# One decoder layer on one core: norm chains of two token tiles, inputs laid out by quarters, and squares added ahead of a sum

## The chip, the core and the metric

The kernel runs on one core of a Trainium2 chip. TensorE (PE in the profile, with its weight loads as PEld) multiplies, VectorE (DVE), ScalarE (ACT) and GpSimd (POOL) do the elementwise work, and SyncE (SP) issues nearly all transfers. The metric is the device time of one launch in microseconds. The kernel before took 1597.15 us, the median of three runs (1595.09 to 1598.02).

## The reference, cut to what matters

The layer has x of 1024 tokens by 1024 columns, in fp32. Only its first stage is touched by most of the change, and the query norm of the memory attention by one line.

```python
def rms_norm(x, gain=None):
    y = x * lax.rsqrt(jnp.mean(x * x, axis=-1, keepdims=True) + EPS)
    return y if gain is None else y * gain

h = rms_norm(x, norm_mix)
rq, rk, rv, rg, dq, dk, dv = split(h @ w_in)
# retention, 8 heads: rotary(rq), rotary(rk), chunks of 128 tokens -> o_ret
dq = rms_norm(dq, diff_q_gain)      # per token and map, 64 columns
dk = rms_norm(dk, diff_k_gain)      # 4 heads, 2 maps each
s  = causal(dq @ dk.T) / 8          # two maps per head
a  = softmax(s[0]) - lam * softmax(s[1])
o_diff = rms_norm(a @ dv, diff_subln) * 0.8
x = x + (concat(o_ret, o_diff) * group_scale) @ w_out

h, m = rms_norm(x, norm_x), rms_norm(mem, norm_mem)
q, (k, v) = h @ xq, split(m @ xkv)
q, k = rms_norm(q, xq_gain), rms_norm(k, xk_gain)   # 4 heads of 256 columns
x = x + softmax(q @ k.T / 16) @ v @ xo
h = rms_norm(x, norm_ffn)
x = x + (silu(h @ w_gate) * (h @ w_up)) @ w_down
```

## The kernel before, in words

Every fp32 operand of a large product is split into a high part, rounded to fp32r by a copy (names with h), and a low part, the rest (names with l). A product is three matmuls, high by high, high by low and low by high (`mm3`). The gain of the first norm goes into the transposed input xT when it is split (`split_x`). The norm's root, one number per token (`rstd`), is not multiplied into xT: it is applied behind the projection.

The projection and both attentions run as one sequence of 64 items, eight groups of eight token tiles (128 tokens each): d0, r0, d1, r1, d2, r2, d3, r3, where d is a differential head (class `Diff`) and r a pair of retention heads (class `Ret`). The loop over n does the attention of item n (`m1`, and the transposes and products of the item before in `m2` and `m3`) and the projection of item n + 4 (`gemm`, in four parts). Between them stand the norm of the queries and keys of a differential tile (`e1`) and the transpose of its keys (`e3`). `e1` sums squares of the keys on ACT and DVE and those of the queries with a matmul by `ones` (tile dss), and then runs `rsqrt`, a chain of 13 DVE instructions on at most 16 columns in which nearly each waits for the one before. Its results are in dsm; rx_d, ry_d and rw_d are the chain's other tiles, rx_x, ry_x and rw_x those of the tokens' root.

Before the loop the kernel loads the input twice: transposed by quarters of 256 tokens, in halves of four blocks (`load_xT`, tiles xs), and by tokens (`load_x`), to get the tokens' root (`token_norm`). For quarters 2 and 3 POOL multiplies the gain in ahead of the split.

All matmuls stay in program order. Where `keep_in_program_order` stands, the other engines do too; elsewhere a scheduler sets an engine's order by priority, and `tc.high_priority()` moves what stands under it ahead. Each engine works through its own queue in that order, so an instruction that waits holds back all behind it. PSUM has two buffers each for projections (mm), scores (S) and small products (ms).

After the loop come the output projection, the memory attention in 16 steps (xG projects two tiles of queries of one head, xR sums their squares and runs `rsqrt`, xS scores, xT_, xO, xX), and the feed-forward part.

## Time and profile before

| | before |
|---|---|
| median of three runs | 1597.15 us |
| profiled execution, its own time | 1599.99 us |
| its span | 1598.2 us |
| mean granted TensorE clock | 0.989 |
| PE busy | 1537.0 us, 96% of the span |
| DVE busy | 1026.7 us, 64% |
| ACT busy | 621.3 us, 39% |
| POOL busy | 280.9 us, 18% |

The profiled execution's own time is 1.8 us above its span, and 2.84 us above the median of the runs. PE is busy nearly everywhere, so the table alone says little: what a change of another engine is worth is read from the stretches in which PE waits for that engine. The page's slices show where these are: the first two slices of 40 (to about 80 us) have the lowest PE share, 6 and 8 tenths, while DVE is at 8 and 9. A granted clock below 1 in a stretch means that matmuls there ran in part at 1.2 instead of 2.4 GHz.

### The profile page before, as it was taken

The page shows a single profiled execution, that of the slowest core. Times are in us where ns is not written, and L with a number is a line of the kernel's source. Part 1 is how long each engine was busy: PE and PEld are TensorE (multiplying, and loading weights), DVE is VectorE, ACT ScalarE, POOL GpSimd, SP SyncE. Part 2 cuts the span into 40 slices and gives each one's busy share as a digit, 9 for nine tenths or more (in the row PEclk, how much of TensorE's full clock was granted, in tenths as well). Part 3 has the DMA queues.
Part 4 walks back from the last instruction along what each step waited for, and adds up shares of the span by engine and source line. Part 5 has one row for each costly group of instructions (what it writes and reads, how often), then busy time and mean ns, then how long its engine had stood idle before and what let it go on. Part 6 is the DMA issues. An engine that isn't in the chain of part 4 may idle for free.

```text
span 1598.2 us, 23419 instructions
## 1 busy us (share of the span) xinstructions
PE 1537.0 (96%) x8782; PEld 1323.4 (83%) x8782; DVE 1026.7 (64%) x2519; ACT 621.3 (39%) x1200; POOL 280.9 (18%) x400
## 2 busy tenths in 40 slices
PE   6899999999999999999999969999999999899999
PEld 6778878888888988899999958888888888688887
DVE  8954864963876734755555886767676666555554
ACT  6442442442445722333332453333333333343332
POOL 3423323322312122111121230000000000000000
PEclk9999999999999999899999999999999999999999
DMA  8201111110103652100001122444444444788562
GB/s 293 73 27 46 39 40 41 40 46 27 41 27 137 208 183 80 40 27 27 27 27 42 79 93 86 152 151 152 163 153 161 166 162 158 250 299 260 199 219 83
DMA packets 69234, 180.85 MB, mean 113 GB/s; under 512 B 7425, under 2 KB 12929, under 8 KB 69121
## 3 DMA queue, kind: packets, MB, share of 16 engines
q1 hardware_dynamic: 68112, 178.81, 31.7%
q8 instruction: 69, 1.13, 0.3%
q10 hardware_dynamic: 1008, 0.55, 0.1%
q14 instruction: 45, 0.36, 0.1%
HBM read 135.55 MB, written 43.78 MB: 112 GB/s over the span
## 4 chain that ended last, share of the span: by engine, by line
PE 80%; DVE 14%; ACT 2%; issue 2%; DMA 1%; POOL 0%; ACTq 0%; SPq 0%; DVEq 0%; POOLq 0%
PE x L64 15%; PE g_r L64 8%; PE z L64 7%; PE dx L64 7%; PE dy L64 6%; PE xo L64 5%; PE wo L64 5%; PE xq L64 5%; PE y L64 4%; PE kv L64 3%; PE xkv L64 2%; PE q L64 2%; PE av L64 2%; DVE nmx L52 2%; DVE dsm L52 1%
## 5 line engine op out<-in xcount | busy, mean ns | idle before, releaser
L64 PE MATMUL g_r<-uh_r,xT 128*128 128x512 f32 x512 | 178.2, 406 | 0.0
L52 DVE TENSOR_TENSOR dl<-ds,dh 128x1024 fp32r<-128x1024 f32 x77 | 94.0, 1224 | 95.4 <-PE dy L64 38.9
L52 ACT CAST dh<-ds 128x1024 fp32r<-128x1024 f32 x77 | 81.0, 1055 | 126.2 <-PE dx L64 63.4
L64 PE MATMUL x<-Bh,f 128*128 128x512 f32 (+1 forms) x368 | 113.7, 381 | 1.2 <-DVE G L52 1.2
L64 PEld LDWEIGHTS g_r<-uh_r,xT 128*128 128x128 f32 x512 | 96.4, 188 | 22.1 <-issue 2.4
L64 PE MATMUL kv<-uh_d,xT 128*128 128x256 f32 x512 | 110.2, 298 | 1.8 <-DVE dql L52 1.8
L52 POOL TENSOR_TENSOR G<-G,U 128x512 f32<-128x512 f32 (+1 forms) x23 | 33.9, 1474 | 395.1 <-ACT f L52 335.1
L52 DVE TENSOR_TENSOR f<-s,f 128x512 fp32r<-128x512 f32 x86 | 70.0, 814 | 50.3 <-ACT f L52 47.4
L64 PE MATMUL g_r<-ul_r,xT 128*128 128x512 f32 x256 | 100.4, 392 | 0.0
L52 ACT CAST f<-s 128x512 fp32r<-128x512 f32 x88 | 54.6, 621 | 115.6 <-DVE s L52 112.9
L64 PE MATMUL xq<-hT,uh_xq 128*128 128x256 f32 x512 | 93.0, 284 | 0.0
L64 PEld LDWEIGHTS kv<-uh_d,xT 128*128 128x128 f32 x512 | 86.2, 195 | 4.5 <-DVE dql L52 2.0
L64 PE MATMUL xo<-uh_xo,xoT 128*128 128x512 f32 x256 | 88.3, 405 | 1.1 <-DVE xr L52 1.1
L52 ACT ACTIVATE p<-s,nmx,dsm 128x128 f32<-128x128 f32 (+7 forms) x64 | 53.2, 831 | 90.1 <-DVE nmx L52 89.2
L64 PEld LDWEIGHTS x<-Bh,f 128*128 128x128 f32 x368 | 68.5, 188 | 14.9 <-DVE G L52 1.8
L64 PEld LDWEIGHTS xq<-hT,uh_xq 128*128 128x128 f32 x512 | 79.8, 191 | 0.1
L64 PE MATMUL kv<-ul_d,xT 128*128 128x256 f32 x256 | 73.6, 287 | 1.1 <-DVE ul_d L52 1.1
L64 PE MATMUL xq<-hT,ul_xq 128*128 128x256 f32 x256 | 72.6, 284 | 0.0
L52 DVE TENSOR_TENSOR G<-x,G 128x512 f32<-128x512 f32 (+1 forms) x69 | 45.7, 663 | 41.8 <-ACT G L52 38.4
L64 PE MATMUL dx<-dl,dh 128*128 128x512 f32 x176 | 68.8, 391 | 2.2 <-DVE dl L52 2.2
L64 PE MATMUL x<-Bl,f 128*128 128x512 f32 (+1 forms) x184 | 69.9, 380 | 0.0
L64 PE MATMUL dx<-dh 128*128 128x512 f32 x176 | 68.7, 390 | 1.1 <-ACT dh L52 1.1
(330 smaller groups left out, 4202.4 us busy)
## 6 DMA issues: line engine op xcount, KB each, us to landing
gu<-in_w_dram SPq DMA_DIRECT2D x21, 1024.0 KB, 6.0
ds<-gF_d SPq DMA_DIRECT2D x77, 256.0 KB, 3.9
wd<-in_w_dram SPq DMA_DIRECT2D x22, 512.0 KB, 5.5
wT_d<-wd SPq DMA_DIRECT2D x22, 512.0 KB, 3.0
ds<-wT_d SPq DMA_DIRECT2D x44, 256.0 KB, 4.1
ds<-in_w_dram SPq DMA_DIRECT2D x33, 256.0 KB, 5.2
st_r<-in_w_dram SPq DMA_DIRECT2D x16, 512.0 KB, 3.2
st_kv<-in_w_dram SPq DMA_DIRECT2D x16, 512.0 KB, 3.8
```

Source lines behind the costliest of these rows:

```text
L52: r = f(*args, **kw)
L64: return tc.keep_in_program_order(nc.tensor.matmul(*args, **kw))
```

## The change

It has four parts.

1. `e1` runs once for two tiles, on eight columns in place of four, and takes its whole chain and the scaling of the keys under `high_priority`. The tokens' root is no longer in it: the norm of a projection does not depend on a factor per token except through EPS, so the chain adds EPS times (mean square of the token + EPS), kept in `epsu`, where it multiplied by `rstd2` and `rstd`. The scaling of the values by `rstd` becomes a step of its own (`e2`), one POOL instruction for two tiles. `e3` does two tiles at once.
2. `token_norm` becomes `token_sum` (ACT's sums of squares and one DVE instruction for `epsu`), and one `rsqrt` over all eight tiles stands in the loop at n = 0. The loads of r0's weights move from n = 0 to n = 1 and 2.
3. The transposed input lies in memory as eight contiguous blocks, one per quarter and half. Its loads and the first weights' keep their order, the first ACT work is a copy of a zeroed tile, the first weight is split in two halves, the high parts of d0's other two weights move from DVE to ACT and one low part from DVE to POOL. POOL's multiplication by the gain goes; all four quarters are split by `activation` and `scalar_tensor_tensor` with the gain.
4. In the memory attention DVE adds the two halves of the queries' squares, and the sum of squares takes two matmuls in place of four.

```diff
-    def rsqrt(ss, n, mean, name, src=None):
+    def rsqrt(ss, n, mean, name, src=None, eps=None):
...
+        if eps is None:
+            ve.tensor_scalar(out=xh, in0=src, scalar1=-0.5 * mean, scalar2=-0.5 * EPS, op0=ALU.mult, op1=ALU.add)
+            ve.tensor_scalar(out=ss, in0=src, scalar1=mean, scalar2=EPS, op0=ALU.mult, op1=ALU.add)
+        else:
+            s3 = ss.rearrange("p (t c) -> p t c", t=2)
+            ve.scalar_tensor_tensor(out=s3, in0=s3, scalar=mean, in1=bc(eps, n // 2), op0=ALU.mult, op1=ALU.add)
+            ve.tensor_scalar(out=xh, in0=ss, scalar1=-0.5, scalar2=None, op0=ALU.mult)
...
-        sp.dma_start(xst[q, j], a["xT"][:, 4 * j:4 * j + 4, 256 * q:256 * q + 256])
-        if q > 1:
-            g = bc(gains[:, G_MIX + 4 * j:G_MIX + 4 * j + 4], 256)
-            for i in range(4):
-                tc.keep_in_program_order(gp.tensor_tensor(out=xst[q, j][:, i:i + 1], in0=xst[q, j][:, i:i + 1],
-                                                          in1=g[:, i:i + 1], op=ALU.mult))
+        tc.keep_in_program_order(nc.sync.dma_start(st, a["xT"][2 * q + j]))
...
-    def token_norm(q):
+    def token_sum(q):
+
         for t in (2 * q, 2 * q + 1):
             xt = xnt.pop(t)
             sc.activation(xt, xt, AF.Square, accum_out=rstd[:, t:t + 1])
-        sl = rstd[:, 2 * q:2 * q + 2]
-        with tc.high_priority():
-            rsqrt(sl, 2, 1.0 / D, f"x{q}")
-        ve.tensor_tensor(out=rstd2[:, 2 * q:2 * q + 2], in0=sl, in1=sl, op=ALU.mult)
+        sl = slice(2 * q, 2 * q + 2)
+        ve.tensor_scalar(out=epsu[:, sl], in0=rstd[:, sl], scalar1=EPS / D, scalar2=EPS * EPS,
+                         op0=ALU.mult, op1=ALU.add)
...
+    gp.memset(Rs[0], 0.0)
+    sc.copy(Rs[1], Rs[0])
+    st0 = raw("st_d0_0")
+    tc.keep_in_program_order(nc.sync.dma_start(st0, a["w"][U_DIF]))
+    w0 = [[uqp.tile([P, 1024], F32R, tag="w", name=f"u{x}_d0_0") for x in "hl"]]
     for j in range(2):
         load_xT(0, j, raw)
+        hi, lo = (t[:, 512 * j:512 * j + 512] for t in w0[0])
+        sc.copy(hi, st0[:, 512 * j:512 * j + 512])
+        low(ve, lo, st0[:, 512 * j:512 * j + 512], hi)
         split_x(0, j)
-    w0 += [unit(U_DIF + i, f"d0_{i}", eng=ve, heng=ve, stage=t4) for i in (1, 2)]
+    w0 += [unit(U_DIF + i, f"d0_{i}", eng=ve if i == 1 else gp, stage=t4, by=ordered) for i in (1, 2)]
...
+            two = slice(t - 1, t + 1)
+            kn = self.kv[:, two, 0:P]
+            for e in range(2):
+                pe.matmul(sp_[:, 2 * e:2 * e + 2], self.q[t // 2][2][:, e * P:e * P + P], ones[:, 0:2],
+                          start=True, stop=True)
...
+            with tc.high_priority():
+                rsqrt(ss, 8, 1.0 / 64, f"d{nm}", eps=epsu[:, two])
+                for e in range(2):
+                    k3 = self.kv[:, t - 1 + e, 0:P].rearrange("p (a d) -> p a d", d=64)
+                    ve.tensor_tensor(out=k3, in0=k3, in1=bc(s3[:, e, 0:2], 64), op=ALU.mult)
+
+        def e2(self, t):
+            if t % 2 == 0:
+                return
+            v = self.kv[:, t - 1:t + 1, P:2 * P]
+            gp.tensor_tensor(out=v, in0=v, in1=bc(rstd[:, t - 1:t + 1], P), op=ALU.mult)
...
         gemm(n + LEAD, (0,))
-        call("e1", n + LEAD - (1 if n else 2))
+        if n % 2 == 0:
+            call("e1", n + LEAD - 1)
+            if n:
+                call("e2", n + LEAD - 1)
         gemm(n + LEAD, (1,))
+        if n % 2:
+            call("e3", n + LEAD - 2)
         if n == 0:
-            call("e3", 0)
-            call("e3", 1)
+            token_sum(2)
+            token_sum(3)
             split_x(3, 1)
-            call("e1", 3)
-            token_norm(3)
+            rsqrt(rstd, NT, 1.0 / D, "x")
+            call("e2", 1)
+            call("e2", 3)
...
-            ws[1] = [load_part(*order[1], i) for i in range(4)]
+        if n in (1, 2):
+            ws.setdefault(1, []).extend(load_part(*order[1], 2 * n - 2 + i) for i in range(2))
...
-        call("e3", n + LEAD - 2)
...
         sc.activation(sq, ps, AF.Square)
+        ve.tensor_tensor(out=sq[:, 0:256], in0=sq[:, 0:256], in1=sq[:, 256:512], op=ALU.add)
...
-            for i in range(2):
-                pe.matmul(sp_[:, e:e + 1], sq[:, 256 * i + e * P:256 * i + e * P + P], ones[:, 2:3],
-                          start=i == 0, stop=i == 1)
+            pe.matmul(sp_[:, e:e + 1], sq[:, e * P:e * P + P], ones[:, 2:3], start=True, stop=True)
```

Three places show how the instructions stand now. The first is ACT's queue at the start of the program, before. uh_d_0 is the high part of the first weight, xs_0 and xs_1 are the halves of the first quarter.

```order
5 L52 DMA tab<-in_tab_dram 128x512
6 L52 DMA causal<-in_causal_dram 128x128
7 L52 DMA zeta<-in_zeta_dram 128x8
8 L52 ACT_TABLE_LOAD
9 L52 CAST uh_d_0_112<-st_d_0_110 128x1024
10 L52 ACTIVATE xT_106<-xs_0_116,gains 128x256 x4
11 L52 ACTIVATE xT_106<-xs_1_126,gains 128x256 x4
12 L52 ACTIVATE negI<-ident 128x128
```

The same queue in the changed program, where R is the zeroed tile:

```order
3 L52 ACT_TABLE_LOAD
4 L52 COPY R_111<-R_110 128x128
5 L52 DMA ones<-in_ones_dram 128x3
6 L52 DMA ident<-in_ident_dram 128x128
7 L52 CAST uh_d_0_116<-st_d_0_114 128x512 x2
8 L52 DMA tab<-in_tab_dram 128x512
9 L52 ACTIVATE xT_106<-xs_0_118,gains 128x256 x4
10 L52 ACTIVATE xT_106<-xs_1_130,gains 128x256 x4
11 L52 CAST uh_d_1_144<-st_d_1_142 128x1024
```

The table load stood directly ahead of the first weight's cast, which needs a transfer; now it stands ahead of a copy that needs none, and the cast of the second weight has come into ACT's queue.

The second place is DVE's queue in group d1, where the norm of tile 4 begins, before. The names with _4 are its chain; aT, rz, cf and p belong to the attention of tiles 0 and 1, and rss and rx_r to the end of retention group r0.

```order
462 L52 TENSOR_REDUCE dsm_4_2247<-dks_4_2248 128x2
463 L52 COPY dsm_4_2247<-dss_4_2245 128x2
464 L52 COPY aT_0_2278<-pt_0_0_2279 128x128
465 L52 TENSOR_SCALAR dsm_4_2247<-dsm_4_2247,rstd_109 128x4
466 L52 RECIPROCAL rz_1_2206<-Z_1_2205 128x2
467 L52 TENSOR_SCALAR rx_d_4_2253<-dsm_4_2247 128x4
468 L52 TENSOR_SCALAR rx_r_2289<-rss_2083 128x16
469 L52 SCALAR_TENSOR_TENSOR cf_1_2207<-Z_1_2205,neglam,rz_1_2206 128x1
470 L52 TENSOR_SCALAR dsm_4_2247<-dsm_4_2247 128x4
471 L52 TENSOR_SCALAR rss_2083<-rss_2083 128x16
```

The chain of tiles 4 and 5 at the same place of the changed program:

```order
325 L52 TENSOR_TENSOR nmx_2_2077<-nmx_2_2077,dsm_3_1917 128x1
326 L52 COPY dsm_5_2118<-dss_5_2115 128x2x2
327 L52 SCALAR_TENSOR_TENSOR dsm_5_2118<-dsm_5_2118,epsu 128x8
328 L52 TENSOR_SCALAR rx_d_5_2123<-dsm_5_2118 128x8
329 L52 TENSOR_SCALAR ry_d_5_2124<-dsm_5_2118 128x8
330 L52 TENSOR_SCALAR ry_d_5_2124<-ry_d_5_2124 128x8
331 L52 TENSOR_TENSOR rw_d_5_2125<-ry_d_5_2124 128x8
332 L52 TENSOR_TENSOR rw_d_5_2125<-rw_d_5_2125,rx_d_5_2123 128x8
333 L52 RECIPROCAL rz_2_2079<-Z_2_2078 128x2
334 L52 SCALAR_TENSOR_TENSOR ry_d_5_2124<-rw_d_5_2125,ry_d_5_2124 128x8
```

The chain's instructions stood every second or third place between others; now they stand nearly side by side, once for two tiles.

The third place is PE's queue at the start of the attention of group d1, before: dkt_1 is the transpose of the keys of tile 1, s_0 are the scores of tile 0, rop_7 the last product of retention group r0.

```order
612 L64 MATMUL rop_7_2078<-R_208,rqT_7_2007 128x128
613 L64 MATMUL rop_7_2078<-rv_7_1691,rsc_7_2063 128x64 x2
614 L68 MATMUL dkt_1_2084<-ident,dkv_1715 128x128
615 L64 MATMUL s_0_0_2092<-dkT_1714,dqh_0_1751 128x128 x2
616 L64 MATMUL s_0_0_2092<-dkT_1714,dql_0_1752 128x128
```

The same place in the changed program, where kv_3 is the projection of tile 3 (seven of its nine rows are left out):

```order
587 L68 MATMUL dkt_1_1847<-ident,dkv_1560 128x128 x2
588 L64 MATMUL rsk_7_1852<-rqT_7_1821,rkT_7_1822 128x128 x2
589 L64 MATMUL kv_3_1834<-uh_d_2_1216,xT_106 128x256
...
597 L64 MATMUL kv_3_1834<-uh_d_2_1216,xT_106 128x256
598 L64 MATMUL rop_7_1870<-R_110,rqT_7_1821 128x128
599 L64 MATMUL rop_7_1870<-rv_7_1536,rsc_7_1855 128x64 x2
600 L64 MATMUL s_0_0_1880<-dkT_1559,dqh_0_1596 128x128 x2
```

The transposes of tiles 0 and 1 now stand together, ahead of the second half of kv_3. The scores of tile 0 read what that pair leaves; before, they read what an earlier transpose of tile 0 alone had left.

## Rows read from the trace of the kernel before

**Rows 1.** Busy time by stretches: us, engines, granted clock, DMA share, GB/s
```profile
0.00:7.64 7.64, 0.00 (x1) 0.00 (x1) 1.03 (x6) 2.79 (x4) 0.53 (x6) 1.00 0.77 241
7.64:20.75 13.11, 11.32 (x74) 10.83 (x75) 12.39 (x27) 9.63 (x24) 1.55 (x3) 1.00 1.06 377
20.75:36.40 15.65, 13.82 (x104) 13.40 (x102) 15.30 (x61) 10.78 (x22) 9.76 (x16) 0.89 0.84 315
36.40:56.14 19.74, 11.34 (x72) 9.92 (x72) 19.40 (x101) 10.29 (x25) 11.29 (x16) 0.83 0.34 120
56.14:103.48 47.34, 45.37 (x288) 37.19 (x289) 38.38 (x133) 21.14 (x52) 13.57 (x21) 1.00 0.10 34
160.00:216.00 56.00, 51.68 (x368) 45.30 (x366) 47.35 (x203) 26.69 (x70) 17.56 (x26) 0.97 0.13 46
286.00:340.00 54.00, 49.85 (x362) 43.57 (x363) 46.55 (x199) 26.12 (x68) 17.12 (x26) 1.00 0.12 44
409.00:462.00 53.00, 49.40 (x350) 43.70 (x349) 45.28 (x199) 24.64 (x65) 13.75 (x21) 0.97 0.08 29
4.84:48.58 43.74, 30.93 (x208) 29.52 (x208) 40.62 (x162) 28.27 (x59) 18.16 (x28) 0.88 0.79 283
```
**Rows 2.** Timeline of PE, 0 to 57 us: start, duration, instruction, [idle before <-releaser]
```profile
7.64 0.58 PE L64 MATMUL q<-xT,uh_d 128*128 128x256 f32 x1 [7.64 <-ACT xT L52]
28.66 0.39 PE L64 MATMUL kv<-uh_d,xT 128*128 128x256 f32 x1 [1.82 <-DVE dql L52]
37.83 0.33 PE L68 MATMUL dkt<-ident,dkv 128*128 128x128 f32 x1 [1.43 <-DVE dkv L52]
43.13 0.58 PE L64 MATMUL dss<-ones,dqs 128*128 128x2 f32 x2 [4.97 <-DVE dkT L52]
50.56 0.50 PE L64 MATMUL s<-dkT,dqh 64*128 64x256 f32 x2 [0.77 <-ACT p L52]
```
**Rows 3.** Waits of PE, 160 to 220 us: total us, times, longest
```profile
PE av L64 <- DVE aT L52: 2.5, 2, 1.5
PE mt L68 <- DVE aT L52: 1.1, 1, 1.1
PE rt L68 <- ACT ro L52: 0.2, 1, 0.2
```
**Rows 4.** Timeline of ACT, 0 to 49 us
```profile
4.84 1.28 ACT L52 ACT_TABLE_LOAD   x1 [4.84 <-DMA st_d<-in_w_dram]
7.08 1.70 ACT L52 ACTIVATE xT<-xs,gains 128x256 fp32r<-128x256 f32 x4
13.51 0.51 ACT L52 ACTIVATE xT<-xs,gains 128x256 fp32r<-128x256 f32 x1 [2.21 <-DMA xs<-in_xT_dram]
39.50 1.98 ACT L52 CAST uh_r<-st_r 128x1024 fp32r<-128x1024 f32 x2
48.58 0.46 ACT L52 ACTIVATE p<-s,nmx,dsm 128x128 f32<-128x128 f32 x1 [7.10 <-DVE nmx L52]
```
**Rows 5.** Timeline of DVE, 195 to 206 us
```profile
196.28 0.16 DVE L52 TENSOR_TENSOR rw_d<-ry_d 128x4 f32<-128x4 f32 x1
196.48 0.16 DVE L52 TENSOR_TENSOR rw_d<-rw_d,rx_d 128x4 f32<-128x4 f32 x1
203.13 0.66 DVE L52 TENSOR_TENSOR rw_d<-rw_d,rx_d 128x4 f32<-128x4 f32 x1
```
**Rows 6.** Timeline of POOL, 160 to 216 us
```profile
202.12 3.04 POOL L52 TENSOR_TENSOR ul_d<-st_d,uh_d 128x256 fp32r<-128x256 f32 x4 [7.40 <-ACT uh_d L52]
```
**Rows 7.** Timeline of PE in the memory attention, 715 to 717 us
```profile
715.63 0.95 PE L64 MATMUL xss<-ones,xsq 128*128 128x1 f32 x8
716.44 0.48 PE L64 MATMUL xo<-uh_xo,xoT 128*128 128x512 f32 x1
```
**Rows 8.** Timeline of ACT in the memory attention, 712 to 716 us
```profile
713.17 0.60 ACT L52 ACTIVATE xsq<-xq 128x512 f32<-128x512 f32 x1
```
**Rows 9.** Chain of waits, 110 to 560 us: one projection of a tile
```profile
157.19 2.88 PE kv L64 x24
```

More of the change, by code (lines that the diff above doesn't have):

```diff
@@ L237, in split_x @@
         hv, o = xT[q // 2], 256 * (q % 2)
-        if q > 1:
-            hi, lo = (hv[:, 4 * j:4 * j + 4, x, o:o + 256] for x in range(2))
-            sc.copy(hi, s3)
-            low(ve, lo, s3, hi)
-            return
         for i in range(4):
@@ L250, in body @@
     rstd = cp.tile([P, NT], F32, tag="rstd", name="rstd")
-    rstd2 = cp.tile([P, NT], F32, tag="rstd2", name="rstd2")
-    def token_norm(q):
+    epsu = cp.tile([P, NT], F32, tag="epsu", name="epsu")
+    def token_sum(q):
         for t in (2 * q, 2 * q + 1):
@@ L367, in e1 @@
             pass
-        e3 = e1
+        e2 = e3 = e1
         def m1(self, n):
@@ L494, in gemm @@
                 sc.copy(self.kv[:, t, :], self.ps[:, 0:256])
-                self.ks[t] = self.kv[:, t, 0:P]
         def e1(self, t):
+            if t % 2 == 0:
+                return
             g = self.g
             nm = f"{g}_{t}"
-            kn = self.ks[t]
+            two = slice(t - 1, t + 1)
+            kn = self.kv[:, two, 0:P]
             sp_ = ms(f"dss{nm}")
-            pe.matmul(sp_[:, 0:2], self.q[t // 2][2][:, (t % 2) * P:(t % 2) * P + P], ones[:, 0:2],
-                      start=True, stop=True)
@@ L505, in e1 @@
-            ss = sm.tile([P, 4], F32, tag="dss", bufs=6, name=f"dsm{nm}")
-            self.ss[t] = ss
-            sk = h5(f"dks{nm}")
-            sc.activation(sk, kn, AF.Square)
-            p64 = lambda ap: ap.rearrange("p (a d) -> p a d", d=64)
-            ve.tensor_reduce(out=ss[:, 0:2], in_=p64(sk), axis=AX.X, op=ALU.add)
-            ve.tensor_copy(ss[:, 2:4], sp_[:, 0:2])
-            ve.tensor_scalar(out=ss, in0=ss, scalar1=rstd2[:, t:t + 1], scalar2=None, op0=ALU.mult)
-            rsqrt(ss, 4, 1.0 / 64, f"d{nm}")
@@ new lines, in e1 @@
+            ss = sm.tile([P, 8], F32, tag="dss", bufs=4, name=f"dsm{nm}")
+            s3 = ss.rearrange("p (t c) -> p t c", t=2)
+            self.ss[t // 2] = s3
+            sk = h1(f"dks{nm}")
+            sc.activation(sk.rearrange("p (t c) -> p t c", t=2), kn, AF.Square)
+            ve.tensor_reduce(out=s3[:, :, 0:2], in_=sk.rearrange("p (t a d) -> p t a d", t=2, a=2), axis=AX.X, op=ALU.add)
+            ve.tensor_copy(s3[:, :, 2:4], sp_[:, 0:4].rearrange("p (t c) -> p t c", t=2))
+            with tc.high_priority():
[3 more added lines that the diff above has]
+                    ve.tensor_tensor(out=k3, in0=k3, in1=bc(s3[:, e, 0:2], 64), op=ALU.mult)
@@ L519, in e3 @@
+        def e2(self, t):
+            if t % 2 == 0:
+                return
+            v = self.kv[:, t - 1:t + 1, P:2 * P]
+            gp.tensor_tensor(out=v, in0=v, in1=bc(rstd[:, t - 1:t + 1], P), op=ALU.mult)
         def e3(self, t):
+            if t % 2 == 0:
+                return
             tp = ms(f"dkt{self.g}_{t}")
-            pe.transpose(tp[:, 0:P], self.ks.pop(t), ident)
-            dst = slice(P * t, P * t + P)
+            for e in range(2):
+                pe.transpose(tp[:, e * P:e * P + P], self.kv[:, t - 1 + e, 0:P], ident)
+            dst = slice(P * (t - 1), P * (t + 1))
@@ L523, in e3 @@
             gk = gx[:, 8:9]
[L524 to L525 removed]
+            sc.activation(self.kT[:, 0, dst], tp[:, 0:2 * P], AF.Copy, scale=gk)
+            ve.scalar_tensor_tensor(out=self.kT[:, 1, dst], in0=tp[:, 0:2 * P], scalar=gk,
                                     in1=self.kT[:, 0, dst].bitcast(F32), op0=ALU.mult, op1=ALU.subtract)
@@ L960, in xR @@
         for e in range(2):
-            for i in range(2):
-                pe.matmul(sp_[:, e:e + 1], sq[:, 256 * i + e * P:256 * i + e * P + P], ones[:, 2:3],
-                          start=i == 0, stop=i == 1)
+            pe.matmul(sp_[:, e:e + 1], sq[:, e * P:e * P + P], ones[:, 2:3], start=True, stop=True)
         rq = small(2, "rq", f"rq{n}")
@@ L1411, in layout @@
     r["x"] = x.reshape(NT, P, D)
-    r["xT"] = x.T.reshape(KB, P, S).transpose(1, 0, 2)
+    r["xT"] = x.T.reshape(2, 4, P, 4, 256).transpose(3, 0, 2, 1, 4).reshape(8, P, 1024)
     r["mem"] = mem.reshape(2, P, D)
```

41 lines of the change are left out of this document (16 added, 25 removed).

## The prediction

> **What bounds the kernel now.** I read the page first for the two slices with a poor PE share, then the busy times by stretch, then PE's own timeline and waits there, and last the queues of the engines that PE waits for.
>
> In the first 56.14 us PE works for 0 + 11.32 + 13.82 + 11.34 = 36.48 us and stands for 19.7; the reader sees beside it that DVE is full (15.30 of 15.65, 19.40 of 19.74) and that the granted clock falls to 0.89 and 0.83 [rows 1]. At a clock of 1 the same matmuls would take about 31 us (my estimate: some 1.9 us lost while the clock starts, 15.65 x 0.11 = 1.7 and 19.74 x 0.17 x about half = 1.7). PE's stops are named: 7.64 us for the first split, then DVE's dql, dkv and dkT (1.82, 1.43, 4.97) and ACT's p (0.77) [rows 2]. So DVE is the limit from 20 to 56 us.
>
> From 56 to 103 us PE stands for only 47.34 - 45.37 = 1.97 us. Then come the stretches in which a differential group takes over from a retention group: PE stands for 4.32, 4.15 and 3.60 us, DVE is busy for 45 to 47 us of 53 to 56, and the clock is 0.97, 1.00, 0.97, which costs 56 x 0.03 = 1.7 and 53 x 0.03 = 1.6 us [rows 1]. In the first of them 3.6 us of the wait are for DVE's copies of aT, only 0.2 for ACT [rows 3]. In the memory attention PE has no such gap: products follow one another directly [rows 7], so there what PE doesn't do is time won.
>
> **Part 1 and 2, the start.** The table load takes 1.28 us and stands behind the wait for the first weight [rows 4]; ahead of a copy of a zeroed tile it runs during the transfer. The first cast then starts near 4.84, not 6.1. A block of a quarter is now one contiguous run per partition in place of four, so SP issues the loads sooner. But the DMA share stands at 1.06 from 7.64 us, so the bytes set the landing [rows 1]: ACT's wait of 2.21 us for the sixth block shows it [rows 4]. I give the transfers 1 us at most.
>
> DVE loses two casts, one low part, the chain of the root for each quarter and half the chains of four tiles; its 40.62 us of work from 4.84 to 48.58 fall to some 31 (estimate: 19 instructions less for each of two pairs and three root chains of 13 at 0.16 to 0.20 make 11 to 14, and four large splits become 16 small ones, which adds about 2). ACT becomes the engine that ends last. It had 28.27 us in that window [rows 1]. It loses the table load (1.28) and two casts of r0's weights (1.98, they stand behind p now), gains two casts of d0's (about 2.0), and sixteen pieces at 1.70/4 = 0.425 replace four casts of 1024 columns at about 1.0 (half of 1.98), which adds 2.8 [rows 4]. That makes 29.8 us, so 4.84 + 29.8 = 34.6, and about 3 us of waits for blocks, for projections and for DVE: p of tile 0 at 37.6 in place of 48.58 [rows 4], 11 us earlier. PE would still stop twice: about 2 us at the pair's transposes, whose chain waits on DVE behind splits and sums that need ACT, and about 3 us for p, since the scores of tile 1 need the two buffers that p frees. Both are in the 37.6. I take **11 us**. Bounds: at best PE is the limit, 7.1 + 31 + 1.9 = 40 against 56.14, so 16; at worst DVE's contiguous chains wait on ACT's sums again and again, which I price at two more waits of 3 us, so 5. What is late next is p behind ACT's squares.
>
> Covered and costed at nothing: the low part that moves to POOL (3.04 us for one such part [rows 6]) needs to be there only for kv_0's second half, piece by piece, and PE reaches that while the pieces come; if that cover is gone it costs PE up to 1 us. r0's weights come later by one or two items; POOL needs four parts of 3 us, from about 40 to 53 us, and their first product stands at n = 4, near 58. From 56 to 103 us I take 1 of the 1.97 us (bounds -1 and 2).
>
> **Part 1, the three later groups.** Per pair DVE had 2 x 18 instructions and has 17, and one dkT in place of two. A dependent step takes 0.16 us and comes each 0.20 [rows 5]; 19 fewer are 3.0 us where they stood alone, about half that where they lay between others. Three pairs fall in each stretch: 4.5 to 9 us less of 45 to 47. The wait that this can remove is 12.07 us less three times 0.2 for ACT, with the clock's 3.3: 14.7 in all. As DVE is freed of more than PE waited for, nearly all could go; but the chain now holds the queue for 13 x 0.20 = 2.6 us and about 1 for its ends, and an aT behind it is late by that. I take three quarters, **11 us**. Bounds: 3 (only the instructions' half price helps, and each pair delays one aT) and 14.7. The added `e2` on POOL is one instruction for two; values are wanted only at the products with aT, more than an item later.
>
> **Part 4.** Four sums in a step stand from 715.63 to 716.44, 0.81 us for eight passes [rows 7]; two take 0.40. Fifteen of sixteen steps lie in a full PE: 15 x 0.40 = **6 us**. DVE's added instruction on 256 columns is bound from below by nothing and from above by 0.60, ACT's time for twice its columns; it can start when ACT's square ends, 713.17 + 0.60, and PE wants it at 715.63 [rows 7, 8], so 1.9 us cover it. Bounds 2 and 6.5.
>
> **The sum.** 11 + 1 + 11 + 6 = 29. Against the profiled execution's own 1599.99 us that is 1571.0; the median of the runs shown stands 2.84 lower, so 1568.
>
> **Rivals.**
>
> *The pairs give the later groups little.* The first tile of a pair waits for the second, and the scores of tile 0 stand one half projection behind the pair's transposes. For it: PE's waits there are short, single ones (the longest 1.5 us [rows 3]), which a queue held for 3.6 us could make anew. Against it: DVE's total, and half a projection, 2.88/2 = 1.4 us [rows 9], between transpose and scores, against about 1 for ACT's and DVE's copies (estimate). The gain falls from 11 to 0 or 3; 1568 + 9 = 1577 to 1579.
> The Trainium skill says against this change, in Perfetto Trace Analysis, section Optimizing Scalar/DVE Operations, that where DVE isn't saturated but makes others wait, breaking up instructions may let work end sooner; the same section says that grouping helps a saturated engine. By the first sentence the groups would give nothing and the time be 1579; by the second, the forecast. The trace bears out the second up to now, with DVE at 47.35 of 56 us.
>
> *The start is half as good.* ACT's queue holds squares, splits and copies in an order fixed ahead, and each may wait for a transfer or a projection. For it: the DMA share of 1.06 and ACT's wait of 2.21 us. Against it: 19 blocks of 0.52 MB at 377 GB/s [rows 1] take 26 us, so all land near 31, ahead of ACT's last squares. The start gives 5 or 6; 1568 + 6 = 1574.
>
> *Slower: POOL's shadow falls on the chains.* While POOL works through a weight's low part, a step of the chain takes 0.66 us in place of 0.20 [rows 5, 6]. The chain now stands ahead of everything and is unbroken; if POOL's pieces fall on it, all of DVE's queue waits. POOL has 17.56 us in a stretch [rows 1]; at 0.66 a step these hold 26 steps that need 5.3 us free, so up to 12 us are lost per group, 49 in four. Less the 18 from start, sums and the middle that is 31 slower at worst; a time of 1597 + 15 = 1612 if half falls so. It decides from the point where the shadow on a pair is longer than the slack between the sum of squares and the transposes: half a query projection, one and a half of keys and values, at 2.88 each [rows 9], and the retention products between, about 6.5 us, against 3.6 of chain, so 2.9 us, for most of the twelve later pairs. Against it: POOL's pieces lay on chains before as well, and there were twice as many steps.
> On the same point the Trainium skill (SBUF — State Buffer, section Who interferes with whom) says that a DVE instruction with two SBUF inputs and a GpSimd instruction that reads SBUF block each other for the whole instruction. The 0.66 beside POOL's work agrees; the rule says no more of where the pieces will fall.
>
> **How the numbers follow.** Forecast 0.58, pairs give little 0.20, start half as good 0.14, slower 0.06, and 0.02 that the parts cancel. A measurement tells this kernel from no change at about 0.2%, 3.2 us. The first three are faster by far more than that: 0.92 faster, 0.02 the same, 0.06 slower. The sums of the bounds are 16 + 2 + 14.7 + 6.5 = 39, 1558, and 5 - 1 + 3 + 2 = 9, 1588. Not all worst ends fall together, so the range is 1557 to 1585; it leaves out the slower case and little else.
>
> **What would show it.** Right: the table load ends before the first weight lands; p of tile 0 at 36 to 40 us; PE's stop for dql gone and that for dkT under 3 us; granted clock 1.00 in the three stretches, with PE waits under 1.5 us each; dss with 2 x 2 columns and 17 DVE instructions per pair; xss with four passes in about 0.4 us and steps of 15.1 us. Wrong: PE waits of over 1 us for dkv, dkT or s in each group, chains at 0.66 us a step under POOL's parts, or p of tile 0 after 44 us.

## The result, and the profile after

The changed kernel takes 1570.76 us (median of 4 runs, 1569.94 to 1571.35) beside 1597.59 of the kernel before (4 runs) on the same chip: a ratio of 0.9831, 95% interval [0.9817, 0.9846]. On a second chip it took 1570.67 (1569.76 to 1572.86). Forecast were 1568, in a range of 1557 to 1585. The profiled execution took 1570.77, its span is 1569.0; before, the profiled execution took 1599.99.

The first view is the table of busy times by stretch, with the columns of [rows 1], of the changed kernel: the start up to the scores of tile 2, the stretch to 89.90, the three stretches where a differential group takes over (each 13.6 to 20 us earlier than in [rows 1]), and ACT's queue from its first cast to p of tile 0 (the exponentials of that tile's scores).
```profile
0.00:6.64 6.64, 0.00 (x0) 0.00 (x0) 1.83 (x8) 3.27 (x6) 0.41 (x5) 1.00 0.71 253
6.64:19.75 13.11, 12.26 (x82) 11.41 (x83) 9.44 (x18) 10.92 (x24) 3.19 (x4) 1.00 1.03 403
19.75:31.00 11.25, 10.73 (x90) 10.47 (x89) 10.10 (x40) 10.94 (x28) 0.00 (x0) 1.00 1.02 404
31.00:41.27 10.27, 9.27 (x76) 8.58 (x74) 9.60 (x55) 8.84 (x25) 1.47 (x3) 1.00 0.30 99
41.27:89.90 48.63, 44.97 (x292) 38.16 (x292) 39.41 (x98) 23.64 (x53) 22.11 (x33) 1.00 0.19 66
146.40:202.40 56.00, 53.67 (x388) 47.43 (x388) 42.30 (x146) 28.14 (x66) 16.37 (x23) 1.00 0.13 44
268.50:322.50 54.00, 51.82 (x375) 45.83 (x374) 41.36 (x142) 27.00 (x64) 16.37 (x23) 1.00 0.12 44
389.00:442.00 53.00, 50.82 (x372) 45.13 (x372) 38.12 (x141) 24.98 (x61) 13.35 (x19) 1.00 0.09 31
4.40:36.06 31.66, 27.64 (x208) 26.13 (x208) 26.16 (x92) 28.61 (x66) 3.19 (x4) 1.00 0.87 342
```
Up to the scores of tile 2 PE stands for 9.0 us (19.7 before) and the granted clock is 1.00 where it was 0.89 and 0.83; PE's busy time there falls from 36.5 to 32.3 us for about as many matmuls. ACT is now fuller than DVE (28.61 against 26.16 of 31.66 us). But PE itself is nearly full: behind its first matmul at 6.64 it stands for 2.4 us, and the scores of tile 2 at 41.27 come 1.3 us behind the 40 that the forecast gave as its best case, with PE as the limit.

PE's timeline shows what is left of its waits; the counterparts are [rows 2, 3].
```profile
6.64 1.10 PE L64 MATMUL q<-xT,uh_d 128*128 128x256 f32 x2 [6.64 <-ACT xT L52]
26.88 0.53 PE L68 MATMUL dkt<-ident,dkv 128*128 128x128 f32 x2 [0.52 <-DVE dkv L52]
36.67 0.50 PE L64 MATMUL s<-dkT,dqh 64*128 64x256 f32 x2 [1.00 <-ACT p L52]
52.18 0.38 PE L64 MATMUL kv<-uh_d,xT 128*128 128x256 f32 x1 [2.19 <-DVE dql L52]
162.50 0.44 PE L68 MATMUL dkt<-ident,dkv 128*128 128x128 f32 x2 [1.49 <-DVE dkv L52]
192.48 0.33 PE L68 MATMUL pt<-ident,p 128*128 128x128 f32 x1 [0.78 <-DVE aT L52]
```
The waits of 4.97 for dkT and 1.82 for dql (the low part of the queries) are gone from the start; a new one of 2.19 for dql stands at 52 us, and one of 1.4 to 1.5 for dkv in each of the three later groups (the others at 283.45 and 404.38).

ACT's timeline answers to [rows 4]: the table load is over before the first weight lands, and p of tile 0 starts at 36.06.
```profile
1.65 1.28 ACT L52 ACT_TABLE_LOAD   x1 [1.65 <-PEq L1471]
4.40 0.62 ACT L52 CAST uh_d<-st_d 128x512 fp32r<-128x512 f32 x1 [1.16 <-DMA st_d<-in_w_dram]
36.06 0.46 ACT L52 ACTIVATE p<-s,nmx,dsm 128x128 f32<-128x128 f32 x1
```
In the memory attention the timeline of DVE and of PE answers to [rows 7]: the added instruction, and the passes, four now.
```profile
687.61 0.48 DVE L52 TENSOR_TENSOR xsq<-xsq 128x256 f32<-128x256 f32 x1
...
689.41 0.50 PE L64 MATMUL xss<-ones,xsq 128*128 128x1 f32 x4
```

Where the time came from, by the first PE instruction of a phase in both traces: to the scores of tile 2, 56.14 to 41.27, gives 14.9 us, 12.5 of them up to p of tile 0 (48.58 to 36.06). From there to the first query projection of the next differential group (140.0 to 126.5) 1.3 are given back. The three groups shrink from 124.99, 123.43 and 124.29 to 121.03, 120.93 and 121.05, 9.7 us. The memory attention from its first query product to the feed-forward (659.26 to 931.67, now 635.97 to 899.72) gives 8.7. In the feed-forward's first half 2.9 are lost: 442.0 us before, 445.0 after.

### The profile page after: what moved, and what is told of

Same layout as the page of the kernel before. It is cut to its first block, busy times and chain, and to the rows that moved or that the text cites. A ratio compares the mean times of both kernels' runs of the same rounds, so it can differ in the third digit from the quotient of the medians.

```text
span 1569.0 us, 22932 instructions
## 1 busy us (share of the span) xinstructions
PE 1524.4 (97%) x8718; PEld 1312.4 (84%) x8718; DVE 984.0 (63%) x2186; ACT 621.9 (40%) x1184; POOL 267.4 (17%) x371
## 4 chain that ended last, share of the span: by engine, by line
PE 84%; DVE 10%; ACT 2%; issue 2%; DMA 1%; POOL 1%; SPq 0%; ACTq 0%; DVEq 0%; POOLq 0%
PE x L64 15%; PE g_r L64 11%; PE z L64 8%; PE dx L64 7%; PE dy L64 6%; PE xo L64 5%; PE wo L64 5%; PE xq L64 5%; PE y L64 4%; PE kv L64 3%; PE av L64 2%; PE s L64 2%; PE q L64 1%; PE xkv L64 1%; PE rsk L64 1%
## 5 line engine op out<-in xcount | busy, mean ns | idle before, releaser
L64 PE MATMUL kv<-uh_d,xT 128*128 128x256 f32 x512 | 104.4, 290 | 2.2 <-DVE dql L52 2.2
L64 PEld LDWEIGHTS kv<-uh_d,xT 128*128 128x128 f32 x512 | 83.0, 191 | 4.7 <-DVE dql L52 2.6
```

Source lines behind the costliest of these rows:

```text
L64: return tc.keep_in_program_order(nc.tensor.matmul(*args, **kw))
```

## Experiments

All are the changed kernel with one edit, except the repeat. Totals spread: single runs of one kernel lie up to 8 us apart (the kernel before, 1593.14 to 1600.93 us on one chip), with the granted clock of a run between 0.986 and 0.998. So the effect of an edit is read at landmarks of the trace: ACT's p of tile 0, the first query projection of the second differential group ("d1"), the groups' lengths. Each trace is one execution; the two of the changed kernel differ by 0.25 us at the first of these landmarks and by 0.35 at the second.

**The repeat.** 

> The changed kernel once more, unchanged, so that the experiments of this chip have it beside them. Every theory: 1569 to 1574, since in the first experiments single runs of one kernel stood up to 6 us apart, with the granted clock between 0.989 and 0.997; the same PE waits at the same places to 0.1 us.

Measured: 1570.67 us; p of tile 0 at 35.81, d1 at 126.82, waits of 2.22, 1.50, 1.40 and 1.40 at the same places. These are the reference below.

**The gain on POOL again.**
```diff
+        if q > 1:
+            g = bc(gains[:, G_MIX + 4 * j:G_MIX + 4 * j + 4], 256)
+            for i in range(4):
+                tc.keep_in_program_order(gp.tensor_tensor(out=xst[q, j][:, i:i + 1], in0=xst[q, j][:, i:i + 1],
+                                                          in1=g[:, i:i + 1], op=ALU.mult))
...
+        if q > 1:
+            sc.copy(hi, s3)
+            low(ve, lo, s3, hi)
+            return
```


> The changed kernel with the gain of the last two quarters of the inputs multiplied by POOL again, each block then split by one large ACT cast and one DVE subtraction, as the kernel before does. It gives DVE 8 instructions less in place of 16 smaller ones, ACT some 2.8 us less and POOL 16 products of 0.7 us beside DVE's first chain. Theory (moving the gain off POOL is a part of the start's gain: POOL's products stretch DVE's steps, and ACT's cast waits for POOL as well as for the transfer): p of tile 0 comes 2 to 5 us later than 36.06; 1573 to 1576. Rival (ACT is the engine that ends last, so fewer and larger ACT instructions help): p of tile 0 comes 1 to 3 us earlier; 1568 to 1570.

Measured: 1575.21 us (1574.37 to 1577.96); p of tile 0 at 41.65, d1 at 131.46, so 5.8 and 4.6 us later. Timeline of this kernel, of POOL, DVE and PE in turn: POOL's products, the first step of DVE's chain, two later ones and the scaling of the keys that ends it, and PE's wait behind them.
```profile
24.51 5.34 POOL L52 TENSOR_TENSOR xs<-xs,gains 128x256 f32<-128x256 f32 x8 [1.79 <-DMA xs<-in_xT_dram]
...
25.87 0.57 DVE L52 SCALAR_TENSOR_TENSOR dsm<-dsm,epsu 128x8 f32<-128x8 f32 x1
27.63 0.53 DVE L52 TENSOR_TENSOR rw_d<-ry_d 128x8 f32<-128x8 f32 x1
30.11 0.17 DVE L52 SCALAR_TENSOR_TENSOR ry_d<-rw_d,ry_d 128x8 f32<-128x8 f32 x1
30.91 0.49 DVE L52 TENSOR_TENSOR dkv<-dkv,dsm 128x128 f32<-128x128 f32 x2
...
31.26 0.69 PE L68 MATMUL dkt<-ident,dkv 128*128 128x128 f32 x2 [4.86 <-DVE dkv L52]
```
The first and the last of these DVE instructions in the changed kernel:
```profile
23.76 0.17 DVE L52 SCALAR_TENSOR_TENSOR dsm<-dsm,epsu 128x8 f32<-128x8 f32 x1
26.53 0.49 DVE L52 TENSOR_TENSOR dkv<-dkv,dsm 128x128 f32<-128x128 f32 x2
```
While POOL works (to 29.85) a step takes 0.53, behind it 0.17. PE's wait of nearly 5 us for DVE, as long as that of [rows 2], is back. The theory holds, a little beyond its 2 to 5 us, and this is the largest single part of the start. The stretching is only a part: the keys are scaled 4.4 us later, of which 2.3 lie in the chain (5.0 us long and not 2.8). The other 2.1 lie ahead of it, where DVE has two subtractions of 1024 columns (1.71 and 1.21) and ACT a cast that waits 0.33 for POOL. Between the keys and p the last 1.4 come, with a granted clock of 0.55 from 32 to 36 us, behind PE's stop.

**The tokens' root again.**
```diff
+        if q < 3:
+            ex = small(2, "exr", f"exr{q}")
+            with tc.high_priority():
+                rsqrt(ex, 2, 1.0 / D, f"e{q}", src=rstd[:, sl])
```


> The changed kernel with one addition: for each of the first three quarters the tokens' root (two columns, 13 dependent DVE instructions with priority) is computed again right behind the sums of squares, as the kernel before had it, into a tile that nothing reads. It shows what leaving these three chains out of the start is worth. Theory (DVE is the limit at the start): 39 instructions at 0.1 to 0.2 us, 4 to 7 us of DVE, of which the two that lie ahead of the pairs' chains make p of tile 0 later than 35.8 to 36.1 by 3 to 5 us; 1574 to 1576. Rival (ACT is the engine that ends last, and DVE's root chains fit in its waits for ACT): p of tile 0 later by less than 1 us; 1570 to 1572.

Measured: 1573.85 us (1572.11 to 1574.40); p of tile 0 at 38.66, d1 at 129.90, 2.9 and 3.1 us later; PE's waits for dkv and p grow to 1.40 and 1.63. Not all of this is the edit's. ACT's cast of the second weight, in the repeat, in this kernel and in that of the next experiment:
```profile
9.65 1.04 ACT L52 CAST uh_d<-st_d 128x1024 fp32r<-128x1024 f32 x1 [0.20 <-DMA st_d<-in_w_dram]
10.92 1.05 ACT L52 CAST uh_d<-st_d 128x1024 fp32r<-128x1024 f32 x1 [1.46 <-DMA st_d<-in_w_dram]
11.20 1.05 ACT L52 CAST uh_d<-st_d 128x1024 fp32r<-128x1024 f32 x1 [1.58 <-DMA st_d<-in_w_dram]
```
In the executions of the two edited kernels, which ran on another chip than the repeat, this weight landed late, behind the same loads in the same order. The first query product of the second quarter, ahead of which neither edit has done anything, stands at 19.80 here and at 18.33 in the repeat, 1.5 us apart. That leaves 1.4 us at p and 1.6 at d1 for the three root chains: less than the theory's 3, more than the rival's 1.

**The first retention weights early again.**
```diff
-        if n in (1, 2):
-            ws.setdefault(1, []).extend(load_part(*order[1], 2 * n - 2 + i) for i in range(2))
```
and, at the end of the block of `n == 0`,
```diff
+            ws[1] = [load_part(*order[1], i) for i in range(4)]
```


> The changed kernel with the four weights of the first retention group loaded and split at item 0 again, as in the kernel before, in place of two at item 1 and two at item 2. Two ACT casts of 1.0 us then stand ahead of p of tiles 0 and 1 and two more between p of tile 1 and dkT; POOL's four low parts come some 3 us earlier. Theory (ACT's order sets the end of the start): p of tile 0 later by 1 us, the scores of tile 2 by 2 to 4 us, and the wait for dql at 52 us shrinks as POOL is done with most of its parts before the chain of tiles 4 and 5; in sum 0 to 3 us, 1571 to 1574. Rival (the place of the casts costs nothing, the shadow is what counts): the wait of 2.2 us goes and nothing comes for it, 1568 to 1569.

Measured: 1574.22 us (1572.89 to 1578.40); p of tile 0 at 39.16 (3.4 later), the scores of tile 2 at 46.91 (5.9 later), the wait for dql gone, d1 at 129.68, so 2.9 later. Of each, 2.4 us stand already at the first query product of the second quarter (20.77 and not 18.33), by the late weight and by a granted clock of 0.73 and 0.84 from 12 to 20 us, ahead of anything that the edit moved. Net of that p comes 0.9 us later and the scores of tile 2 come 3.5 later, as the theory says, and d1 0.4: what moving these casts behind p paid, the wait at 52 us that it brought took back nearly whole.

**The old layout of the inputs.**
```diff
-        tc.keep_in_program_order(nc.sync.dma_start(st, a["xT"][2 * q + j]))
+        tc.keep_in_program_order(nc.sync.dma_start(xst[q, j], a["xT"][:, 4 * j:4 * j + 4, 256 * q:256 * q + 256]))
```


> The changed kernel with the inputs' old layout in memory: each block of a quarter is four runs of 1 KB for a partition in place of one of 4 KB; order of the loads and all else as changed. Theory (bytes set the landing, not the number of pieces): p of tile 0 within 0.5 us of 36.06, the first matmul within 0.3 of 6.64; 1571. Rival (pieces count): each block lands later by some share, the blocks of the later quarters come 3 us late in sum, p of tile 0 at 38 to 39; 1573 to 1575.

Measured: 1571.98 us (1570.44 to 1573.19); the first matmul at 7.62 in place of 6.70, p of tile 0 at 37.08, d1 at 128.12. Both readings miss: the pieces cost 0.9 us at the first matmul, 1.3 at p and d1. The blocks land more slowly throughout (346 to 388 GB/s in the stretches of 4 us from 4 to 28 us, 400 to 409 in the repeat), but behind the first weights no engine waits for a transfer: the first blocks are late and all follows.

**The table load behind the first weight again.**
```diff
-    sc.copy(Rs[1], Rs[0])
+    gp.memset(Rs[1], 0.0)
```


> The changed kernel with ACT's first copy of a zeroed tile taken out (POOL zeroes both), so that the activation table's load stands behind the wait for the first weight again. Theory (the load is on the path to the first matmul): the first matmul starts 1.0 to 1.3 us later than 6.64, and 0.5 to 1.3 of that is left at tile 0's p (36.06); time 1571 to 1572. Rival (transfers set the time from the third block on, so the load is hidden): the first matmul 1 us later, p of tile 0 within 0.3 us.

Measured: 1574.67 us (1571.48 to 1576.31); the first matmul 0.4 us later (7.14), p of tile 0 at 38.18, d1 at 129.03, 2.2 us later. Neither reading holds. The edit also made the scheduler put ACT's casts and squares in another order, and PE then waits 1.75 for dkv and 1.37 for p. How much is the 1.28 us of the load alone stays open.

**Two chains for a pair.**
```diff
-                rsqrt(ss, 8, 1.0 / 64, f"d{nm}", eps=epsu[:, two])
                 for e in range(2):
+                    rsqrt(ss[:, 4 * e:4 * e + 4], 4, 1.0 / 64, f"d{nm}_{e}", eps=epsu[:, t - 1 + e:t + e])
```


> The changed kernel with one root chain of width 4 for each of the two tiles of a pair in place of one of width 8; the pair's sums, transposes and values stay as they are, and the tokens' own root stays out. It adds some 11 to 13 dependent DVE instructions per pair at 0.20 us, 2.4 us for each pair. Theory (DVE's length of chain is what makes PE wait in the differential groups): tile 0's p comes 1 to 3 us later than 36.06, each of the three later groups loses 2 to 4 of the gain of 3.3 us, since PE's waits for dkv grow from 1.4 by up to 2.4 in each pair; 1570.8 + 8 to 14, so 1579 to 1585. Rival (DVE has slack again and the width gave nothing; moved transposes and the tokens' root gave the gain): within 2 us of 1570.8.

Measured: 1578.21 us (1573.99 to 1580.08); the trace is of the fastest execution. Busy times over a whole differential group, first of the kernel before, its first two later groups (the third has 124.29 and 120.40 of PE).
```profile
140.04:265.03 124.99, 120.60 (x811) 104.88 (x810) 82.50 (x312) 49.84 (x124) 38.25 (x63) 0.99 0.11 40
265.03:388.46 123.43, 119.00 (x812) 103.30 (x810) 82.20 (x312) 49.64 (x124) 38.22 (x63) 1.00 0.12 41
```
The same of the changed kernel, its first later group (the others have 120.93 and 121.05, with PE at 118.63 and 118.66).
```profile
126.47:247.50 121.03, 118.64 (x811) 103.71 (x809) 71.31 (x232) 48.96 (x116) 36.41 (x59) 1.00 0.12 41
```
And of the kernel with two chains (the others 122.47 and 122.67).
```profile
127.70:250.16 122.46, 119.30 (x811) 103.88 (x810) 74.04 (x284) 49.16 (x116) 35.61 (x59) 1.00 0.12 41
```
DVE has 312, 232 and 284 instructions in a group. PE stands for 4.39, 2.39 and 3.16 us; the rest of the difference is PE's busy time. With two chains that is 0.7 us longer at a granted clock of 1.00 in both, for a reason that these rows don't show. The width of 8 is worth 1.5 us for a group, 4.6 of the 9.7: between theory and rival, since the longer chain adds a wait for dkv (0.56) in the first pair of a group alone. At d1 it is 0.9, but 0.7 of them stand at the first query product of the second quarter already (19.04), ahead of the first chain. The other 5.1 us of the groups (the tokens' root out of the chain, the pair's transposes, the values on POOL) were not undone on their own.

**The finish one item later.**
```diff
-        run_fin()
+        if n % 16 or not n:
+            run_fin()
```


> The changed kernel with one edit: in the items n = 16, 32 and 48 the retention's finishing step is not called, so it comes one item later, and its reduction, root steps and POOL products no longer stand between the steps of the first new pair's chain in each later group. Theory (the remaining wait of 1.4 to 1.5 us at the first dkt of each later group is that finish, its DVE instructions of 1.2 us and POOL's rg*ro beside the chain): the three waits go, 3 x 1.4 = 4 us less, 1566 to 1567, and the chain's last steps take 0.2 us in place of 0.5 to 0.7. Rival (the finish only moves the shadow to the next pair's chain): the wait stands at the next dkt with about the same length, 1569 to 1572. A time above 1573 would say that the group's finish was needed where it stood.

Measured: 1585.10 us (1580.38 to 1586.60). The waits for dkv are gone and the chain's steps take 0.17, as the theory says; but the finish now lies ahead of an aT, and PE waits 2.9 us for that in each group. PE's timeline at the first and the third of these waits:
```profile
178.51 0.94 PE L64 MATMUL av<-dkv,aT 128*128 128x128 f32 x6 [2.91 <-DVE aT L52]
426.87 1.65 PE L64 MATMUL av<-dkv,aT 128*128 128x128 f32 x6 [2.91 <-DVE aT L52]
```
The busy times of the same kernel behind them, with the granted clock third from the end of a row:
```profile
178.50:182.00 3.50, 3.49 (x24) 2.96 (x25) 2.47 (x7) 0.37 (x1) 0.00 (x0) 1.00 0.14 55
426.80:430.30 3.50, 3.43 (x18) 2.92 (x18) 1.23 (x4) 0.37 (x1) 0.00 (x0) 0.50 0.15 59
430.30:434.30 4.00, 4.00 (x18) 3.23 (x17) 2.75 (x10) 1.25 (x3) 0.00 (x0) 0.66 0.00 0
```
The same wait is followed by a clock of 1.00 in the first group and of 0.50 (1.2 GHz) in the third, so the same six products take 0.94 and 1.65. The groups last 123.41, 124.94 and 127.90 (in the third PE also waits 1.51 for POOL's rkz near the end): the finish was needed where it stood.

**Part 4 undone.**
```diff
-        ve.tensor_tensor(out=sq[:, 0:256], in0=sq[:, 0:256], in1=sq[:, 256:512], op=ALU.add)
...
-            pe.matmul(sp_[:, e:e + 1], sq[:, e * P:e * P + P], ones[:, 2:3], start=True, stop=True)
+            for i in range(2):
+                pe.matmul(sp_[:, e:e + 1], sq[:, 256 * i + e * P:256 * i + e * P + P], ones[:, 2:3],
+                          start=i == 0, stop=i == 1)
```


> The changed kernel with part 4 alone undone: each query step of the memory attention takes its sums of squares from four one-column passes again, and DVE's addition is gone. Theory (the passes are pure PE time in a full PE): 15 or 16 steps x 0.40 us = 6.0 to 6.4 us more than the changed kernel's 1570.8, so 1577, all of it between the first xo (670.2 in the changed kernel) and the last xq (868.3), with the three attention groups and the start as they are in the changed kernel. Rival (the clock, not the passes, gave the 8.3 us that this part of the trace shows): the time rises by 2 or less, or by 8 and more; then the granted clock of 670 to 870 us differs between the two. A second thing to be read: the changed kernel lost about 3 us where the memory attention hands over to the feed-forward; if part 4 brought that about, the step at the hand-over is back at the kernel before's, and the total rises by 3 only.

Measured: 1578.28 us (1575.58 to 1579.04), 7.6 more. From the first xo to the feed-forward it takes 235.66 us and the kernel before 235.74; the changed kernel takes 229.56, the repeat 230.58. So 5.1 to 6.1 lie there, nearly what the theory says. The rest stands between the first xq and the first xo. Busy times of that stretch in the kernel before, in this one and in the changed kernel:
```profile
659.26:695.93 36.67, 32.97 (x241) 32.24 (x240) 21.46 (x61) 13.29 (x29) 4.59 (x5) 0.86 0.09 29
637.40:674.03 36.63, 32.95 (x241) 32.23 (x240) 21.43 (x61) 13.27 (x29) 4.57 (x5) 0.86 0.08 29
635.97:670.16 34.19, 30.51 (x233) 29.79 (x232) 21.90 (x63) 13.27 (x29) 4.57 (x5) 0.90 0.09 31
```
Two of the sixteen steps lie in that stretch, some 0.9 us. The wait for hT is the same (3.23 to 3.25); the rest is the granted clock behind it, as the rival says. Whether part 4 has to do with that clock is open: the two kernels without it took 36.6 and 36.7 us there, all ten traces of kernels with it 32.9 to 34.3 (32.9 at a clock of 1.00), but each is one execution. In sum, from the first xq to the feed-forward, part 4 undone costs 8.1 to 8.5 us, nearly all of the 8.7 that the memory attention gained. The feed-forward's first half takes 443.5 us here, 442.0 before and 442.9 to 445.1 in the ten traces, so its loss is not shown to be part 4's.

**Shadow taken away.** Both edits were chosen after the traces above.
```diff
-            return unit(U_RET + 4 * g + i, f"r{g}_{i}", eng=gp, pool=up if i else uqp, pin=True)
+            return unit(U_RET + 4 * g + i, f"r{g}_{i}", eng=ve if g == 0 and i < 2 else gp, pool=up if i else uqp, pin=True)
...
-                for c in cut4(1024):
-                    gp.tensor_tensor(out=rg[:, c], in0=rg[:, c], in1=o[:, c], op=ALU.mult)
             def f3(last):
-                ve.tensor_tensor(out=p64(o), in0=p64(rg), in1=bc(ss, 64), op=ALU.mult)
+                ve.tensor_tensor(out=p64(rg), in0=p64(rg), in1=bc(ss, 64), op=ALU.mult)
+                ve.tensor_tensor(out=o, in0=o, in1=rg, op=ALU.mult)
```


> The changed kernel with two edits that take POOL's work away from DVE's chains. First, the low parts of the first two weights of the first retention group are made by DVE (2 x 1.2 us) and not by POOL (5.76 us beside the chain of tiles 4 and 5). Second, the retention's finish multiplies gate by root and by output on DVE, after its root, so POOL's four products (2.81 us beside the last steps of the first new pair's chain) are gone and DVE has 1.21 us more. Theory (the steps stretched by POOL's work set the remaining waits): the wait of 2.19 us for dql at 52 us falls below 0.5, and the three waits of 1.4 to 1.5 for dkv fall below 0.3, since the stretched steps cost about 1.5 us each time; together 5 to 6 us, 1565 against 1571. Rival (what stands between the steps holds the chain, not their stretching; or DVE's added 1.21 us makes aT late, as when the finish was moved by one item): the waits for dkv stay above 1 us or come back at av as 1 to 3 us; 1570 to 1578.

Measured: 1565.12 us (1562.69 to 1566.79), ratio to the kernel before 0.9797 [0.9775, 0.9818]; beside the repeat's 1570.67 (from 1569.76) no run overlaps. First the changed kernel, POOL and DVE in the start and then in the first later group:
```profile
41.96 5.76 POOL L52 TENSOR_TENSOR ul_r<-st_r,uh_r 128x256 fp32r<-128x256 f32 x8
45.69 0.67 DVE L52 TENSOR_SCALAR rx_d<-dsm 128x8 f32<-128x8 f32 x1
46.27 0.78 DVE L52 TENSOR_SCALAR ry_d<-dsm 128x8 int32<-128x8 int32 x1
51.65 0.48 DVE L52 SCALAR_TENSOR_TENSOR dql<-q,gains,dqh 128x256 fp32r<-128x256 f32 x1
...
155.72 1.21 DVE L52 TENSOR_REDUCE rss<-rsq 128x16 f32<-128x1024 f32 x1
158.10 1.22 DVE L52 SCALAR_TENSOR_TENSOR rg<-rsq,rg 128x1024 f32<-128x1024 f32 x1
159.40 2.81 POOL L52 TENSOR_TENSOR rg<-rg,ro 128x256 f32<-128x256 f32 x4 [6.71 <-DVE ry_d L52]
159.43 0.72 DVE L52 TENSOR_TENSOR rw_d<-ry_d 128x8 f32<-128x8 f32 x1
161.81 0.75 DVE L52 TENSOR_TENSOR dkv<-dkv,dsm 128x128 f32<-128x128 f32 x2
```
Then the same places of the kernel with the two edits, again the timeline, where DVE does what POOL did, with one wait of PE:
```profile
42.09 2.76 DVE L52 TENSOR_TENSOR ul_r<-st_r,uh_r 128x1024 fp32r<-128x1024 f32 x2
46.95 0.17 DVE L52 TENSOR_SCALAR rx_d<-dsm 128x8 f32<-128x8 f32 x1
48.33 0.48 DVE L52 SCALAR_TENSOR_TENSOR dql<-q,gains,dqh 128x256 fp32r<-128x256 f32 x1
55.81 0.94 PE L64 MATMUL av<-dkv,aT 128*128 128x128 f32 x6 [1.24 <-DVE aT L52]
...
158.51 0.17 DVE L52 TENSOR_TENSOR rw_d<-ry_d 128x8 f32<-128x8 f32 x1
159.57 0.49 DVE L52 TENSOR_TENSOR dkv<-dkv,dsm 128x128 f32<-128x128 f32 x2
```
And the busy times of its first later group:
```profile
125.64:244.99 119.35, 118.45 (x811) 103.70 (x810) 70.69 (x233) 48.96 (x116) 33.52 (x55) 1.00 0.12 42
```
dql is ready 3.3 us earlier and its wait is gone; two waits for aT (0.71 and 1.24, where the changed kernel has one of 0.69) take part of it back, so d1 comes 1.2 us earlier. The waits for dkv are gone, PE stands for 0.90 us of a group in place of 2.39, and each group is 1.6 us shorter. Theory, 5.5 us of the 5 to 6: rss and rg still stand between the chain's steps, so the stretching by POOL set these waits. This version beats both kernels.

## Why the prediction was right, and where its terms were off

**What bounds the kernel.** Right in the main: DVE's chains ahead of the pair's transposes and ahead of p set the start, and once DVE is relieved ACT is the fuller of the two ([rows 1, 2, 4] against 28.61 of 31.66). That PE itself is then nearly full stood in the forecast as its best case only.

**Start, 11 forecast, 14.9 measured.** The 11 were worked out at p of tile 0, where 12.5 came; the other 2.4 lie between p and the scores of tile 2, a stretch that the sum took as unchanged. The step that was mis-sized is the split of the last two quarters. It was priced as a cost, 2.8 us on ACT and about 2 on DVE for sixteen small pieces, and of POOL's work only the added low parts were looked at. That the sixteen products which leave POOL had stood beside DVE's chains was not priced, although [rows 5, 6] show such a step at 0.66: undone, this edit costs 5.8 us at p of tile 0, 2.3 of them by stretched steps. The other parts, undone, cost there 1.4 (roots) and 0.9 (r0's casts), net of the late weight, and 1.3 (layout, against at most 1). At d1, net of what stood at the first query product of the second quarter already (but for the layout and the table load, whose edits act ahead of it), the six undone parts (4.3, 2.2, 1.6, 1.3, 0.4, 0.2) add to 10.0, against 13.6 measured for start and middle together. Where the other 3.6 come from is not shown: the casts that moved from DVE to ACT, the halved first weight and the pair's transposes were not undone on their own, and most of these edits also change the order that the scheduler gives ACT's and DVE's queues. Of the waits put into the 37.6, that at the pair's transposes is 0.52 and not 2, and that for p 1.00 and not 3.

**Middle, +1 forecast, -1.3 measured.** The step "POOL needs four parts of 3 us, from about 40 to 53 us" had the time right and asked only whether its product is late, not what lies beside it: the chain of tiles 4 and 5, whose steps take 0.53 to 0.78 there. dql stands behind most of its steps, which cost the 2.19.

**Three groups, 11 forecast, 9.7 measured.** Mechanism right: by the tables of whole groups PE's stops fall from 4.2 to 2.4 us in a group, 5.6 in all, and 4.1 come from PE's busy time. Some 3.3 of these are the clock's, as forecast (an estimate: the kernel before was granted 0.57 in the 4 us from 180.04 and 0.61 in those from 428.46, the changed one 1.00 throughout). What was forecast as a held queue and a late aT (the quarter taken off) is 0.78 us in each group; the rest is the wait for dkv in POOL's shadow. With it, signs of both kinds came: 1.40 to 1.49 us is under the 1.5 that was to show the forecast right, and over the 1 us for dkv in each group that was to show it wrong, and the chain's last steps take 0.51 to 0.72 beside POOL's products. The version without POOL's products shows what that was worth, 1.6 us of a group.

**Part 4, 6 forecast, about 8 measured.** Four passes take 0.50 us at 689.41 where eight took 0.95 [rows 7]; steps come each 15.02 us where they came each 15.49, so a step gives 0.45 to 0.47 and not 0.40, and all sixteen give it, some 7.2. DVE's addition takes 0.48 at 687.61, and its pass comes at 689.41: the cover held. Undone, part 4 costs 8.1 to 8.5; the 1 us or so beyond the passes is the clock ahead of the first xo, whose cause is open. The 2.9 lost at the feed-forward are the clock's: PE's waits in its first half add to 9.1 us before and 9.0 after, and its busy time for the same 1991 matmuls is 432.9 and 436.0, since 1.2 GHz is granted for other lengths of time behind the waits. The changed kernel has 0.66, 0.84 and 0.50 in the three stretches of 5 us from 909.72, 924.72 and 929.72; the kernel before has 1.00, 0.67 and 0.65 in those of the same work.

**The rivals.** The slower one named the right mechanism: POOL's shadow did fall on chains, in one pair of the start and the first pair of each later group. It cost about 5.5 us in all, by the version without it, and not the 15 of that rival, since elsewhere POOL's parts miss the chains or the slack covers them. Its premise was wrong: "the chain now stands ahead of everything and is unbroken". Built without the priority, every engine has the same instructions in the same order as with it; the scheduler fills the gaps between dependent steps with whatever is ready, rss and rg among it. The fixed order of the first loads likewise moves nothing: without it SP's loads stand in the same order. So both of these parts are worth nothing here. The Trainium skill's sentence on breaking up instructions (Perfetto Trace Analysis, section Optimizing Scalar/DVE Operations) is not borne out for the chains: two narrow ones cost 1.5 us for a group.

**The level.** The sum of 29 fits the two profiled executions, 29.2, but by luck: the start gave 3.9 more than forecast and the memory attention 2.7 more, the middle 2.3 and the groups 1.3 less, and the feed-forward lost 2.9 that stood in no term. The medians are only 26.8 apart: 2.84 us were taken off because the profile of before stood above its median, but the low clock of that run was also in the terms (the 3.3 of the groups). So a part of the gain read there was this run's own. That reading of the miss of 2.8 us is argued, not tested.
